# Interleaving the DRAM operands of an RWKV-7 mixer's batches, and loading them several tiles per transfer

## The chip, the cores and the metric

The kernel runs on one NeuronCore of a Trainium2 chip, with its five instruction streams: TensorE (PE, whose weight loads the profile lists apart as PEld), VectorE (DVE), ScalarE (ACT), GpSimd (POOL) and SyncE (SP), which in this kernel issues nearly all DMAs. Sixteen DMA engines move the data. The metric is the device time of one execution in microseconds (us); smaller is better. Everything below is float32 (or its rounded form fp32r for the large matmuls).

## What is computed

Two layers of a streaming encoder are run for two request groups (a prompt of 16 learned tokens and 1024 others, and a sample of 64 tokens), which the kernel puts side by side as T = 1104 token columns. Layer 0 mixes tokens with a gated DeltaNet, layer 1 with RWKV-7 time mixing; after each mixer stands a SwiGLU block. The change is in layer 1's mixer alone. Its reference, cut to what matters:

```python
def rwkv_mixer(h, shift_buf, S0, mu, w0, ..., w_r, w_k, w_v, w_o, ln_w, ln_b):
    ...
    r, k, v = xr @ w_r, xk @ w_k, xv @ w_v
    ...
    def step(S, inp):
        d_t, kk_t, b_t, v_t, k_t, r_t = inp
        sa = jnp.einsum('bhij,bhj->bhi', S, -kk_t)
        S = S * d_t[:, :, None, :] + sa[..., :, None] * b_t[:, :, None, :] + v_t[..., :, None] * k_t[:, :, None, :]
        return S, jnp.einsum('bhij,bhj->bhi', S, r_t)
    S, y = lax.scan(step, S0.astype(f32), seq)
    ...
    bonus = jnp.sum(r * k * r_k, axis=-1, keepdims=True) * v
    y = y + bonus.reshape(B, T, D)
    y = (y * gate).astype(h.dtype) @ w_o
```

There are 16 heads of 64 features. The kernel doesn't scan token by token; it works in chunks of 64 tokens, with a triangular inverse per chunk and head.

## The kernel before, in words

Features lie on the 128 partitions: a feature tile f (0 to 7) holds two heads, one in partitions 0 to 63 (q = 0) and one in 64 to 127 (q = 1). Tokens lie along the free dimension, in three groups g of six chunks, 384 columns each. A **batch** is one group g with four feature tiles (hf = 0 or 1), so there are six batches, numbered 0 to 5, each of two halves of three chunks.

Layer 1's mixer runs in two parts. In `rwkv_a` four dense projections are computed, with 24 steps (8 feature tiles by 3 groups) each. What follows a step of the projection for k is `post_k` (line 1347): it loads A and the summed decays (tiles `l0` and `sw`), computes the scaled operands, and stores four tiles of 128 x 384 to DRAM: `PQ` (line 1371), `KR[0]` (1373), `BK[0]` = bh (1376) and `BK[1]` = kh (1378). Its tiles have two buffers each. What follows a step of the projection for v is `post_v` (line 1401): it loads pq, kh and rt (1405 to 1407), stores `KR[1]` (1409), `V` (1415) and `BV` (1417). Beside the second of these the first batch is prepared already (lines 1423 to 1427).

In `rwkv_b` the batches follow each other. In the weave of batch i (line 1775) run: `chain(i)`, the recurrence over the six chunks (line 1631); `build` of both halves of batch i + 1 (line 1487); `inverse(i + 1)` (line 1537); `grams(i + 2)` (line 1469), which feeds the inverse after it; and `tail(i - 1)` (line 1688), which norms, adds the bonus, multiplies by the gate and by w_o and adds to x. Batch 0 is different: it has three halves of `build` (0,1), (1,0) and (1,1), `grams(1)` with `inverse(1)`, and the gates of `gates` (line 1093), whose results are stored to `GT` at line 1119.

- `build`, for each of its four feature tiles: six transfers of half the partitions each (four for `bk`, which puts b and k of three chunks side by side, in swapped order in the two halves, line 1503; two for `kb`, line 1505) and one for V (line 1506). Then small matmuls (lines 1512, 1514) whose results DVE masks (1517, 1518); then six matmuls by the identity that turn b and k to token-major (line 1524, copied by ACT at 1525); then six that turn V (line 1531, copied into W by ACT at 1534).
- `inverse`: two copies on ACT and two on DVE gather the 32 x 32 blocks into `rdp`, a tile of its own (line 1543); DVE transposes it into `b32a` (line 1546); 31 steps of substitution follow on DVE with a share on POOL (lines 599, 601); DVE transposes the result twice, into a tile of the slot `b32b` (line 1552) and one of the slot `b32a` (line 1555); then for two sets of blocks come matmuls at line 1567, an ACT copy (1571), matmuls at line 1578 that read the `b32b` tile, and an ACT copy (1581).
- `tail`: it loads `BV` and `GT` (lines 1697, 1699), and for each of the eight output tiles x (line 1726), adds, and stores x (line 1733), as long as g is 0 or 1.

**What sets the order.** `weave` takes steps of its generators in turn by their weights, which gives the program order. The framework that builds the program then moves instructions of an engine against each other where data allow, so the order that ran is the trace's: the `rdp` copies of one inverse, for example, ran ahead of the last matmuls of the inverse before it. Each engine, and SP's queue, then goes strictly in that order: an SP transfer that waits for its data holds up all that are queued behind it. A slot with one buffer (`bufs=1`) can be written for its next use only when the last reader of its former use has ended.

Of the kernel before, what the change touches and what calls it, by code (L numbers as in the profile page):

```python
# [52 lines left out]
def tile_trunk(ctx, tc, *aps, stages=("gdn", "ffn0", "rwkv", "ffn1"), dbg=None):  # L53
# [1039 lines left out]
    def gates(tp, xp, dr):  # L1093
# [18 lines left out]
        for f in range(8):  # L1112
            for g, (c0, n) in enumerate(LIVE):
# [5 lines left out]
                nc.sync.dma_start(dr["GT"][f, :, (g + 1) * 384 - n:(g + 1) * 384], o[:, :n])  # L1119
# [26 lines left out]
    def rwkv_a(hnp, col, prm, pc, plb, dr, esb, esx, esg, pend, esP):  # L1146
        C = math.exp(-0.5)
        with ExitStack() as es0, ExitStack() as es:
# [198 lines left out]
            def post_k(ps, n, g, f):  # L1347
# [28 lines left out]
                nc.sync.dma_start(dr["BK"][0, f, :, cs], bh)  # L1376
                nc.vector.tensor_tensor(kh, k2, pi, ALU.mult)
                nc.sync.dma_start(dr["BK"][1, f, :, cs], kh)
# [16 lines left out]
            with ExitStack() as es, ExitStack() as es1:  # L1395
# [5 lines left out]
                def post_v(ps, n, g, f):  # L1401
# [4 lines left out]
                    nc.sync.dma_start(kh, dr["BK"][1, f, :, cs])  # L1406
# [10 lines left out]
                    nc.sync.dma_start(dr["BV"][f, :, cs], pq)  # L1417
# [27 lines left out]
    class batches:  # L1445
        def __init__(self, dr, tm):
# [8 lines left out]
            self.dp = tm.tile([P, 32, 32], F32, tag="rdp", bufs=1, name="rdp")  # L1455
            nc.gpsimd.memset(self.dp[:, 24:32], 0.0)
# [12 lines left out]
        def grams(self, i):  # L1469
# [3 lines left out]
            for ff in range(4):  # L1473
# [3 lines left out]
                nc.sync.dma_start(b1, self.dr["BK"][0, f, :, cs])  # L1477
# [9 lines left out]
        def build(self, i, half):  # L1487
# [4 lines left out]
            W = B["W"][half] = tz.tile([P, 2, 3, 4, 64], F32, tag=f"W{z}", bufs=1, name=uid("W"))  # L1492
            for ff in range(4):
                f = 4 * hf + ff
                kb = tz.tile([P, 2, 2, 192], F32, tag=f"kb{z}", bufs=4, name=uid("kb"))
# [3 lines left out]
                bk = tp.tile([P, 3, 2, 64], F32, tag="bk", bufs=3, name=uid("bk"))  # L1499
                V = tp.tile([P, 192], F32, tag="V", bufs=2, name=uid("V"))  # L1500
                for q, r in enumerate(HR):
                    for a in range(2):
                        nc.sync.dma_start(bk[r, :, a ^ q], self.dr["BK"][a, f, r, cs].rearrange("p (c t) -> p c t", t=64))
                for q, r in enumerate(HR):
                    nc.sync.dma_start(kb[r, q], self.dr["KR"][:, f, r, cs].rearrange("a p c -> p a c"))
                nc.sync.dma_start(V, self.dr["V"][f, :, cs])
# [15 lines left out]
                for j in range(3):  # L1522
                    for a in range(2):
                        nc.tensor.matmul(v[HR[a], j], bk[:, j, a], ident, start=True, stop=True)
                nc.scalar.copy(bt, v)
                yield
                ps = psB()
                for j in range(3):
                    c = slice(64 * j, 64 * j + 64)
                    for q, r in enumerate(HR):  # L1530
                        nc.tensor.matmul(ps[HR[1 - q], c], V[:, c], ident[:, r], start=True, stop=True)
# [427 lines left out]
```

## Time and profile before

| What | Value |
|---|---|
| Median of 3 runs | 3365.65 us (3364.24, 3365.65, 3377.66) |
| Span of the profiled execution, first to last instruction | 3360.1 us; the profile has nothing of what lies around it |
| PE, PEld, DVE, ACT, POOL busy | 94%, 89%, 76%, 46%, 11% of the span |
| Granted TensorE clock, mean | 0.968 |
| DMA: packets, bytes, mean rate | 543,905, 452.36 MB, 135 GB/s |
| SP's DMA queue, share of 16 engines | 43.1% |

A busy PE isn't a PE at its peak, since the ends of matmuls are modelled. A matmul of float32 appears as two MATMUL rows. Lines in the profile are those of the listing above; where a helper issues an instruction (lines 109 and 110 split a tile into two fp32r parts, 130 to 132 are the three matmuls of a split product), the line is the helper's. By the lines of the trace, the steps of `post_k` lie between about 1792 and 1919 us, those of `post_v` between 1919 and 2079, and the batches' weaves between about 2077 and 2560.

### The profile page before, as it was taken

Reading aid. Unit: us, or ns where it says so; the run is one execution under the profiler, and the core shown is the slowest. Engines: PE = TensorE matmul, PEld = TensorE weight load, DVE = VectorE, ACT = ScalarE, POOL = GpSimd, SP = SyncE. Lnnn points to the kernel's source line nnn. Section 1 sums busy time; section 2 is a strip of 40 time slices with the busy share of each in tenths; the row PEclk is TensorE's granted clock in tenths of the full one; section 3 lists DMA queues with packets and bytes.
Section 4 is the critical chain, followed back from the end, with each engine's and each line's share of the span. In section 5 each row is a group of like instructions: output and inputs, shape, how many; then the busy total and the mean of one; then the engine's idle time right before and its main releaser. Section 6 shows DMA issues by size and latency. Waiting matters only on the chain. (4 is left out here: it accounts for less than half of the span.)

```text
span 3360.1 us, 67649 instructions
## 1 busy us (share of the span) xinstructions
PE 3175.1 (94%) x26274; PEld 2982.5 (89%) x26274; DVE 2553.9 (76%) x5127; ACT 1557.9 (46%) x3134; POOL 383.9 (11%) x719
## 2 busy tenths in 40 slices
PE   7999999899899999999999889889999999999998
PEld 7888888798899999999988777777778999999998
DVE  6968778566787667766887883899976787877775
ACT  5765757444543333212687743444455443333112
POOL 1202022001300000000001130433300310000000
PEclk9989989899999999999999999898999999999999
DMA  5433432694332223522255877455555333325231
GB/s 167 114 91 89 113 89 76 221 301 147 114 107 84 78 78 125 169 79 89 75 172 168 289 232 238 136 152 157 167 188 179 105 96 95 95 92 177 85 98 61
DMA packets 543905, 452.36 MB, mean 135 GB/s; under 512 B 78377, under 2 KB 494930, under 8 KB 543458
## 3 DMA queue, kind: packets, MB, share of 16 engines
q1 hardware_dynamic: 538682, 445.61, 43.1%
q8 instruction: 207, 3.39, 0.4%
q10 hardware_dynamic: 4904, 2.43, 0.3%
q14 instruction: 112, 0.92, 0.1%
HBM read 306.86 MB, written 141.07 MB: 133 GB/s over the span
## 5 line engine op out<-in xcount | busy, mean ns | idle before, releaser
L311 PE MATMUL psA<-tc,sh 128*128 128x276 f32 (+1 forms) x1712 | 499.1, 292 | 19.0 <-DVE hs L319 9.4
L313 PE MATMUL psA<-tc,sl 128*128 128x276 f32 (+1 forms) x1712 | 498.7, 291 | 4.0 <-DVE sl L110 3.9
L312 PE MATMUL psA<-tc,sh 128*128 128x276 f32 (+1 forms) x1712 | 498.3, 291 | 0.3 <-DVE tc L110 0.2
L407 DVE TENSOR_TENSOR xT<-xT,psA 128x384 f32<-128x384 f32 (+3 forms) x496 | 252.9, 521 | 137.0 <-PE psA L132 135.2
L311 PEld LDWEIGHTS psA<-tc,sh 128*128 128x128 f32 x1712 | 326.0, 190 | 21.2 <-DVE hs L319 10.0
L109 ACT CAST wh<-raw 128x1024 fp32r<-128x1024 f32 x159 | 166.2, 1048 | 365.8 <-PE psA L131 269.7
L313 PEld LDWEIGHTS psA<-tc,sl 128*128 128x128 f32 x1712 | 325.3, 190 | 4.9 <-DVE sl L110 4.7
L312 PEld LDWEIGHTS psA<-tc,sh 128*128 128x128 f32 x1712 | 325.5, 190 | 1.2 <-DVE tc L110 0.9
L131 PE MATMUL psA<-hl,wh 128*128 128x384 f32 (+3 forms) x1024 | 326.4, 319 | 0.0
L130 PE MATMUL psA<-hh,wh 128*128 128x384 f32 (+3 forms) x1024 | 325.7, 320 | 0.0
L132 PE MATMUL psA<-hh,wl 128*128 128x384 f32 (+3 forms) x1024 | 325.3, 318 | 0.0
L130 PE MATMUL psA<-hnh,wh 128*128 128x384 f32 (+1 forms) x768 | 270.2, 352 | 5.4 <-ACT hnh L109 4.1
L131 PE MATMUL psA<-hnl,wh 128*128 128x384 f32 (+1 forms) x768 | 269.3, 351 | 2.0 <-DVE hnl L110 2.0
L132 PE MATMUL psA<-hnh,wl 128*128 128x384 f32 (+1 forms) x768 | 267.2, 348 | 0.0
L109 ACT CAST sh<-raw 128x512 fp32r<-128x512 f32 x202 | 124.6, 620 | 253.8 <-PE psA L312 237.8
L130 PE MATMUL psA<-mxh,wh 128*128 128x384 f32 (+1 forms) x672 | 223.4, 343 | 9.9 <-ACT mxh L109 5.6
L110 DVE TENSOR_TENSOR wl<-raw,wh 128x1024 fp32r<-128x1024 f32 x159 | 195.5, 1231 | 47.1 <-ACT wh L109 46.8
L131 PE MATMUL psA<-mxl,wh 128*128 128x384 f32 (+1 forms) x672 | 228.4, 342 | 2.8 <-DVE mxl L110 2.5
L132 PE MATMUL psA<-mxh,wl 128*128 128x384 f32 (+1 forms) x672 | 225.9, 338 | 0.8 <-DVE wl L110 0.8
L130 PEld LDWEIGHTS psA<-hh,wh 128*128 128x128 f32 x1024 | 192.1, 188 | 0.6 <-ACT hh L109 0.4
L132 PEld LDWEIGHTS psA<-hh,wl 128*128 128x128 f32 x1024 | 192.5, 188 | 0.1
L131 PEld LDWEIGHTS psA<-hl,wh 128*128 128x128 f32 x1024 | 192.3, 188 | 0.3
(480 smaller groups left out, 8342.3 us busy)
## 6 DMA issues: line engine op xcount, KB each, us to landing
raw<-in_ffn_w_gate_dram SPq DMA_DIRECT2D x64, 512.0 KB
raw<-in_ffn_w_up_dram SPq DMA_DIRECT2D x64, 512.0 KB
raw<-in_ffn_w_down_dram SPq DMA_DIRECT2D x44, 512.0 KB
raw<-in_gdn_w_in_dram SPq DMA_DIRECT2D x32, 512.0 KB
raw<-in_gdn_w_out_dram SPq DMA_DIRECT2D x24, 512.0 KB
raw<-in_rwkv_w_o_dram SPq DMA_DIRECT2D x24, 512.0 KB
hr<-dhid SPq DMA_DIRECT2D x44, 276.0 KB
hr<-dhid SPq DMA_DIRECT2D x44, 272.0 KB
```

Of the source, the lines that this page charges most:

```text
L109: nc.scalar.copy(h, src)
L110: (eng or nc.vector).tensor_tensor(l, src, h.bitcast(F32), ALU.subtract)
L130: nc.tensor.matmul(ps, w[0][:, k, :], x[0][:, k, :n], start=a, stop=False)
L131: nc.tensor.matmul(ps, w[0][:, k, :], x[1][:, k, :n], start=False, stop=False)
L132: nc.tensor.matmul(ps, w[1][:, k, :], x[0][:, k, :n], start=False, stop=z)
L311: nc.tensor.matmul(ps, u[0][:, kk], h, start=first and kk == 0, stop=False)
L312: nc.tensor.matmul(ps, u[0][:, kk], l, start=False, stop=False)
L313: nc.tensor.matmul(ps, u[1][:, kk], h, start=False, stop=last and kk == 3)
L407: nc.vector.tensor_tensor(xT[:, m, a:a + n], xT[:, m, a:a + n], pd[:, :n], ALU.add)
```

## The change

1. **b and k interleaved in DRAM.** `BK` was [2, 8, 128, 1152] (b or k; tile; partition; token). It becomes [8, 128, 18, 2, 64]: for each chunk of 64 tokens b and k stand next to each other, in swapped order for the upper half of the partitions, as `build` wants them. A store of bh or kh in `post_k` becomes two stores of 64 partitions, each of six runs of 256 bytes a partition; the load of kh in `post_v` and that of b in `grams` become two such loads each.
2. **`build` loads several tiles at a time.** `bk` and V are loaded for two feature tiles per transfer (V has a second small transfer that repeats its first 64 columns at the end), `kb` for all four feature tiles of a half in four transfers of half the partitions.
3. **Transpose mode.** b and k are turned by three 128 x 128 transposes instead of six matmuls; V by three instead of six; ACT copies V's result in three pieces instead of two.
4. **`BV` and `GT` become one DRAM tile `BG`**, which `tail` loads with one transfer for two tiles.
5. **`tail` moves x two tiles at a time**, and a store is issued one step later.
6. **`rdp` loses its own tile.** It takes the slot `b32b`, and its last part is cleared by POOL in every inverse.

The diff, cut to its core:

```diff
@@ post_k
-                nc.sync.dma_start(dr["BK"][0, f, :, cs], bh)
+                for q, r in enumerate(HR):
+                    nc.sync.dma_start(dr["BK"][f, r, 6 * g:6 * g + 6, q], c3(bh)[r])
                 nc.vector.tensor_tensor(kh, k2, pi, ALU.mult)
-                nc.sync.dma_start(dr["BK"][1, f, :, cs], kh)
+                for q, r in enumerate(HR):
+                    nc.sync.dma_start(dr["BK"][f, r, 6 * g:6 * g + 6, 1 - q], c3(kh)[r])
@@ post_v
-                    nc.sync.dma_start(kh, dr["BK"][1, f, :, cs])
+                    for q, r in enumerate(HR):
+                        nc.sync.dma_start(c3(kh)[r], dr["BK"][f, r, 6 * g:6 * g + 6, 1 - q])
@@ batches
-            self.dp = tm.tile([P, 32, 32], F32, tag="rdp", bufs=1, name="rdp")
-            nc.gpsimd.memset(self.dp[:, 24:32], 0.0)
@@ grams
-                nc.sync.dma_start(b1, self.dr["BK"][0, f, :, cs])
+                for q, r in enumerate(HR):
+                    nc.sync.dma_start(b1[r].rearrange("p (c t) -> p c t", t=64), self.dr["BK"][f, r, 6 * g:6 * g + 6, q])
@@ build
+            kbs = tz.tile([P, 4, 2, 2, 192], F32, tag=f"kb{z}", bufs=1, name=uid("kb"))
+            for q, r in enumerate(HR):
+                for a in range(2):
+                    nc.sync.dma_start(kbs[r, :, q, a], self.dr["KR"][a, f0:f0 + 4, r, cs].rearrange("f p c -> p f c"))
             for ff in range(4):
+                if ff % 2 == 0:
+                    fs = slice(f0 + ff, f0 + ff + 2)
+                    bks = tp.tile([P, 2, 384], F32, tag="bk", bufs=2, name=uid("bk"))
+                    nc.sync.dma_start(bks, self.dr["BK"][fs, :, 6 * g + 3 * half:6 * g + 3 * half + 3]
+                                      .rearrange("f p c a t -> p f (c a t)"))
+                    Vs = tp.tile([P, 2, 256], F32, tag="V", bufs=2, name=uid("V"))
+                    v = self.dr["V"][fs, :, cs].rearrange("f p c -> p f c")
+                    nc.sync.dma_start(Vs[:, :, 0:192], v)
+                    nc.sync.dma_start(Vs[:, :, 192:256], v[:, :, 0:64])
...
                 for j in range(3):
-                    for a in range(2):
-                        nc.tensor.matmul(v[HR[a], j], bk[:, j, a], ident, start=True, stop=True)
+                    nc.tensor.transpose(v[:, j], bk[:, j].rearrange("p a t -> p (a t)"), ident)
...
                 for j in range(3):
-                    c = slice(64 * j, 64 * j + 64)
-                    for q, r in enumerate(HR):
-                        nc.tensor.matmul(ps[HR[1 - q], c], V[:, c], ident[:, r], start=True, stop=True)
-                for q in range(2):
-                    o = HR[1 - q]
-                    nc.scalar.copy(W[o, q, :, ff], ps[o, :192].rearrange("p (c t) -> p c t", t=64))
+                    nc.tensor.transpose(v[:, j], V[:, 64 * j:64 * j + 128], ident)
+                nc.scalar.copy(W[0:64, 1, :, ff], v[0:64, :, 64:128])
+                nc.scalar.copy(W[64:128, 0, 1:3, ff], v[64:128, 0:2, 0:64])
+                nc.scalar.copy(W[64:128, 0, 0, ff], v[64:128, 2, 0:64])
@@ inverse
+            dp = tp.tile([P, 32, 32], F32, tag="b32b", bufs=1, name=uid("rdp"))
+            nc.gpsimd.memset(dp[:, 24:32], 0.0)
@@ tail
-                    nc.sync.dma_start(bv[:, :n], dr["BV"][f, :, cs])
-                    nc.sync.dma_start(gt[:, :n], dr["GT"][f, :, cs])
+                    nc.sync.dma_start(bg[:, :, :n], dr["BG"][:, f, :, cs].rearrange("a p c -> p a c"))
...
+                    if g < 2:
+                        xt = tp.tile([P, 2, 384], F32, tag="xt", bufs=2, name=uid("xt"))[:, :, :n]
+                        nc.sync.dma_start(xt, dr["X"][:, xs, c0:c0 + n])
...
+                        if late:
+                            nc.sync.dma_start(*late)
+                            late = None
                         yield
+                    if g < 2:
+                        late = dr["X"][:, xs, c0:c0 + n], xt
```

More of the change, by code (lines that the diff above doesn't have):

```diff
@@ L1695, in tail @@
                     f = 4 * hf + ff
[L1696 to L1699 removed]
+                    bg = tp.tile([P, 2, 384], F32, tag="lbg", bufs=lb, name=uid("lbg"))
+                    nc.sync.dma_start(bg[:, :, :n], dr["BG"][:, f, :, cs].rearrange("a p c -> p a c"))
                     pc_ = psC()
@@ L1721, in tail @@
                     wv = [t.rearrange("p (k m) c -> p k m c", m=2) for t in u]
-                    for mm in range(2):
-                        m = 2 * mp + mm
-                        if g < 2:
-                            xt = tp.tile([P, 384], F32, tag="xt", bufs=4, name=uid("xt"))[:, :n]
-                            nc.sync.dma_start(xt, dr["X"][:, m, c0:c0 + n])
-                        else:
-                            xt = xT[:, m, c0:c0 + n]
+                    xs = slice(2 * mp, 2 * mp + 2)
+                    if g < 2:
+                        xt = tp.tile([P, 2, 384], F32, tag="xt", bufs=2, name=uid("xt"))[:, :, :n]
+                        nc.sync.dma_start(xt, dr["X"][:, xs, c0:c0 + n])
+                    else:
+                        xt = xT[:, xs, c0:c0 + n]
+                    for mm in range(2):
                         ps = psC()
                         mm3(ps[:, :n], (wv[0][:, :, mm], wv[1][:, :, mm]), yy, range(4), n)
-                        nc.vector.tensor_tensor(xt, xt, ps[:, :n], ALU.add)
-                        if g < 2:
-                            nc.sync.dma_start(dr["X"][:, m, c0:c0 + n], xt)
+                        nc.vector.tensor_tensor(xt[:, mm], xt[:, mm], ps[:, :n], ALU.add)
+                        if late:
+                            nc.sync.dma_start(*late)
+                            late = None
                         yield
+                    if g < 2:
+                        late = dr["X"][:, xs, c0:c0 + n], xt
+                if late:
+                    yield
+                    nc.sync.dma_start(*late)
             def first(tp, hp):
@@ L1906, in tile_trunk @@
     if "rwkv" in stages:
-        rs_ = {k: dp_.tile([8, P, 1152], F32, name="r" + k) for k in ("V", "GT", "BV", "R")}
-        for k in ("KR", "BK"):
+        rs_ = {k: dp_.tile([8, P, 1152], F32, name="r" + k) for k in ("V", "R")}
+        rs_["BK"] = dp_.tile([8, P, 18, 2, 64], F32, name="rBK")
+        for k in ("KR", "BG"):
             rs_[k] = dp_.tile([2, 8, P, 1152], F32, name="r" + k)
```

26 lines of the change are left out of this document (9 added, 17 removed).

## The prediction

> **What bounds the kernel now.** I read the page first, then the busy time by stage, then each stage's own limit.
>
> ```profile
> span 3360.1 us, 67649 instructions
> PE 3175.1 (94%) x26274; PEld 2982.5 (89%) x26274; DVE 2553.9 (76%) x5127; ACT 1557.9 (46%) x3134; POOL 383.9 (11%) x719
> ```
>
> PE at 94% is a mean over stages; what the change touches lies between 1792 and 2485 us. The stage table has, for each stretch, the busy us of PE, PEld, DVE, ACT and POOL, then the granted clock, the DMA engines' share and GB/s:
>
> ```profile
> 1792.00:1858.00 66.00, 64.11 (x344) 57.06 (x345) 64.33 (x121) 61.13 (x131) 12.78 (x17) 1.00 0.63 204
> 1858.00:1911.40 53.40, 51.43 (x278) 46.64 (x277) 48.55 (x90) 41.79 (x87) 6.39 (x13) 1.00 0.88 289
> 1925.00:2077.00 152.00, 135.96 (x1124) 117.49 (x1122) 101.70 (x203) 57.56 (x115) 30.34 (x63) 0.99 0.79 242
> 2077.00:2183.00 106.00, 90.98 (x1591) 74.54 (x1589) 76.21 (x181) 45.06 (x105) 36.89 (x81) 0.86 0.51 147
> 2183.00:2476.00 293.00, 265.92 (x4703) 219.80 (x4703) 272.62 (x638) 130.95 (x290) 97.21 (x201) 0.94 0.53 153
> ```
>
> The reader is to see five stages with different limits. In the first stretch of `post_k` PE and DVE are both at 97%. In its second (13 of its 24 steps) PE is at 96%, and the DMA engines at 88%. In `post_v` nothing is full (PE 89%, DMA 79%). In batch 0 (2077 to 2183) nothing is full either: PE is busy for 91 of 106 us, at a clock of 0.86. From 2183 on, batches 1 to 4, DVE is busy for 272.6 of 293 us in 638 instructions: what is left is 32 ns for each, so DVE hardly waits. Its waits there, longest first:
>
> ```profile
> DVE mb L1517 <- PE psB L1514: 2.8, 4, 1.1
> DVE b32a L1546 <- PE psB L1567: 1.9, 2, 0.9
> DVE xt L1731 <- PE psC L132: 1.7, 5, 0.6
> ```
>
> None of them names a DMA. The change takes nothing off DVE, so there its large saving on SP and its saving on PE mostly fall beside the path.
>
> **The change, part by part.** The prices of an issue on SP are these (ns: least, median, most):
>
> ```profile
> L1503 SPq DMA_DIRECT2D bk<-rBK x192: 573/606/1930, 1940.1 to 2462.8; - x192
> L1378 SPq DMA_DIRECT2D rBK<-kh x24: 320/407/580, 1807.2 to 1918.6; - x24
> L1406 SPq DMA_DIRECT2D kh<-rBK x24: 319/406/582, 1920.2 to 2062.7; - x24
> L1505 SPq DMA_DIRECT2D kb<-rKR x64: 573/607/1800, 2081.6 to 2449.7; - x64
> L1506 SPq DMA_DIRECT2D V<-rV x48: 319/537/1777, 1960.4 to 2468.7; - x48
> ```
>
> A transfer over half the partitions (bk, kb) takes 0.61 us, one over all of them 0.40 to 0.54.
>
> *`build` on SP.* A half of a batch issues 4 x (4 x 0.606 + 2 x 0.607 + 0.537) = 16.7 us. Afterwards it issues four of kb at 0.607, two of bk and four of V at 0.32 to 0.54 (I take 0.43): 5.0 us. That is 11.7 us less, 140 us over twelve halves. Where this counts is batch 0, which has three halves (35 us less of SP in 106). There SP goes from one issue to the next with gaps of 0.04 to 0.1 us:
>
> ```profile
> 2143.40 1.73 SPq L1503 DMA_DIRECT2D bk<-rBK  x2
> 2145.23 0.54 SPq L1119 DMA_DIRECT2D rGT<-go  x1
> 2145.82 0.58 SPq L1503 DMA_DIRECT2D bk<-rBK  x1
> 2146.44 1.26 SPq L1505 DMA_DIRECT2D xT<-rKR  x2
> ```
>
> *The transposes.* The rows are start and duration; what a burst costs PE is the distance to the next row's start:
>
> ```profile
> 136.10 0.49 PE L797 MATMUL psB<-ident,sil 128*128 128x128 f32 x3
> 136.34 0.40 PE L131 MATMUL psA<-hnl,wh 128*128 128x336 f32 x1
> ...
> 2488.22 0.88 PE L1524 MATMUL psB<-ident,bk 128*64 128x128 f32 x12
> 2488.93 0.52 PE L1531 MATMUL psB<-ident,V 128*64 128x64 f32 x12
> 2489.27 0.64 PE L1648 MATMUL psA<-W,kb 128*64 128x64 f32 x16
> ```
>
> Line 797 is three transposes of this size elsewhere in the kernel: 0.24 us. The two bursts they replace take 0.71 and 0.34. So a tile and half saves 1.05 - 2 x 0.24 = 0.57 us of PE: 27 us over 48, of which 6.8 in batch 0 (12 of them), 18 in batches 1 to 4, 2.3 in `post_v`.
>
> *Batch 0's sum.* Below: nothing, if its latencies set its length. Above: PE is left with 91.0 - 6.8 = 84.2 us; if it then ran without a gap, 22 us are gained. I take 10, the PE saving and 3 us of late operands: PE's waits there that name SP's loads or no releaser at all (an operand's landing, I take it) are these.
>
> ```profile
> PE psB L1531 <- issue: 2.7, 2, 1.7
> PE psB L1483 <- DMA k<-rKR: 1.0, 2, 0.7
> ```
>
> *Batches 1 to 4.* Only what DVE waits for PE can come back, 6.4 us in the rows above: from 0 to 6, I take 3.
>
> *`post_k` pays.* One step on SP, with the first store of the next:
>
> ```profile
> 1874.65 0.32 SPq L1371 DMA_DIRECT2D rPQ<-pq  x1
> ...
> 1876.04 0.40 SPq L1378 DMA_DIRECT2D rBK<-kh  x1
> ...
> 1876.99 0.44 SPq L1351 DMA_DIRECT2D sw<-rSW  x1
> 1878.47 0.32 SPq L1371 DMA_DIRECT2D rPQ<-pq  x1
> ```
>
> SP is taken for 2.8 us (1874.65 to 1877.43) in a step that lasts 53.4 / 13 = 4.1 in this stretch. Two issues of 0.40 become four of 0.61: 1.6 us more, 4.4 in all, over 4.1. Ahead of the two loads there are now 1.6 us more of stores. The DMA engines, too, get more to do:
>
> ```profile
> DMA packets 11209, 15.41 MB, mean 289 GB/s; under 512 B 1236, under 2 KB 11205, under 8 KB 11205
> q1 hardware_dynamic: 11205, 15.36, 87.5%
> ...
> DMA packets 539, 0.14 MB, mean 39 GB/s; under 512 B 535, under 2 KB 539, under 8 KB 539
> q1 hardware_dynamic: 539, 0.14, 17.1%
> out_dram<-so SPq DMA_DIRECT2D x1, 128.0 KB
> ```
>
> The first two rows are the 53.4 us of these 13 steps: 0.875 x 16 x 53.35 us / 11,205 = 66.7 ns a packet, nearly all of 1.5 KB. The last three are 3.5 us around a lone store of 256-byte rows: 0.171 x 16 x 3.5 us / 539 = 17.8 ns a packet. A step's 256 packets of 1536 bytes (17.1 us of engine time) become 1536 of 256 bytes (27.3): 0.64 us more over 16 engines, which brings 87.5% of 4.1 us to 4.2 us, 103%. So both SP and the DMA engines pass the step's length by 0.1 to 0.3 us: 4 us over the 13 steps. The other 11 steps are longer (the ten in the first stretch take 6.6 us) and have room. Bounds: nothing, if the loads are ordered ahead of the stores and the tiles' second buffers absorb it; 24 x 1.6 = 39 us, if all comes in series. I take 7: the 4, and some of the later loads.
>
> The Trainium skill, "DMA: Bandwidth & Descriptors", section Specifications, says that transfers below 512 bytes aren't at line rate because the DMA engine then reads, modifies and writes. The row of the lone store shows 17.8 ns for 256 bytes against 66.7 for six times as much: less efficient by 1.6, with no second pass to be seen.
>
> *`post_v`.* kh costs SP two issues of 0.61 for one of 0.41, 0.8 us in each of 24 steps, b1 likewise in eight of its 24 uses, and `build` (0,0) gives back 11.7 there. DVE's product waits for pq and rt, which stand beside kh in the queue. From 8 us gained (PE's 2.3 and half of the 11.7) to 19 lost; I take 2 lost, as SP has idle time here and PE 11%.
>
> *The slot of `rdp`.* At the handover from batch 3 to 4:
>
> ```profile
> 2391.33 1.67 ACT L1543 COPY rdp<-at 32x768 f32<-32x768 f32 x2
> 2395.64 1.11 DVE L1543 COPY rdp<-at 32x768 f32<-32x768 f32 x2
> 2402.56 0.95 PE L1567 MATMUL psB<-b32tn,at 32*32 32x32 f32 x48
> 2403.55 2.09 DVE L1546 STREAM_TRANSPOSE b32a<-rdp 128x1024 f32<-128x1024 f32 x1 [0.94 <-PE psB L1567]
> 2406.56 0.95 PE L1578 MATMUL psB<-b32tt,v 32*32 32x32 f32 x48
> ```
>
> The copies ran 8 us and more ahead, and the transpose waited only for line 1567 (the other slot). Now the copies must wait for the end of line 1578 at 2407.5, the last reader of `b32b`; with ACT's two, 1.67 us side by side with DVE's 1.11, the transpose comes at 2409.2: 5.7 us later. Queued behind DVE's copies are all of DVE's masks and the tail's additions, unless ordered ahead. There are four such handovers, 23 us if DVE stood still. DVE has other work, by its rows at least half of the stretch, so I take 8. If the filling work is ready, nothing is lost.
>
> *The rest at nothing.* ACT's third copy (48 more, ACT under 50% busy), POOL's clearing (POOL busy 97 of 293), `tail`'s fewer transfers and later stores (SP only, under a DVE that is full). If that cover were gone, the copies would cost 48 times some 0.2 us, 10 us.
>
> Sum: -10 - 3 + 7 + 2 + 8 = +4 us. The profiled span of 3360.1 lies 5.6 below the median of the runs, 3365.65, with nothing shown of what lies around it; I add the sum to the median: **3370 us**.
>
> **The rivals.** A measurement of this kernel can tell about 0.5%, 17 us, from no change.
>
> *Two: SP's queue is what holds the batches.* For it: SP's back-to-back issues, and that batch 0 is the longest though no engine is full. Then batch 0 gains the 22, batches 1 to 4 the 6, the handovers and `post_v` come free, and 7 are paid: -21, 3345. Against it: few waits name a DMA.
>
> *Three, slower: `post_k` becomes bound by its stores.* It decides where SP's 4.4 us pass the step's 4.1. If the loads stand behind the four half stores in every step, the whole 1.6 us come in series: 39 in place of 7, 3402. Against it: double buffers, and ten steps with room.
>
> *Four: a 256-byte store costs twice*, 35.6 ns, because its bytes move twice. Then 13 steps hold 13 x (54.7 - 17.1) / 16 = 30.6 us more of DMA time on 46.7, 77 us for 53.4: +24 in place of 7, 3387. The lone store speaks against it. It is what the rule of the Trainium skill above (same page and section) would give.
>
> *Five: the handovers cost their full 23*, +15 over mine: 3385. For it: DVE's order is fixed, so a copy that waits stops DVE.
>
> **How the numbers follow.** Forecast 0.45, two 0.27, three 0.13, four 0.03, five 0.12. The forecast's own range is where its terms stay within the bounds of no change, 3350 to 3382. Two lies faster by over 0.5% (3349). Three and four lie above 3382; five straddles it, 0.07 above. Faster 0.27, same 0.50, slower 0.23. The range reaches down past two's 3345, and up through five to half of three: 3338 to 3392.
>
> **What would show it.** Right: batch 0 about 96 us instead of 106; a step of `post_k` at 4.3 to 4.9 us instead of 4.1, DMA share there over 0.93, SP back to back; the transposes 0.25 us a burst of three; line 1546 waiting for ACT's or DVE's copies after line 1578. Wrong: `post_k`'s stretch at its old length (then SP and DMA had room), batches 1 to 4 shorter by over 10 us (then DVE wasn't the bound), or 256-byte stores well over 18 ns.

## The result, and the profile after

The changed kernel takes 3471.52 us (median of 4 runs, 3470.92 to 3476.48), the kernel before on the same chip 3366.11 (4 runs, 3364.24 to 3377.66). The ratio is 1.0293, with a 95% interval of 1.0273 to 1.0313: about 105 us slower, where 4 us were forecast and the range ended at 3392.

The page of the kernel after, its first lines:

```profile
span 3469.6 us, 65672 instructions
...
PE 3204.5 (92%) x25410; PEld 2994.8 (86%) x25410; DVE 2553.2 (74%) x5127; ACT 1563.2 (45%) x3182; POOL 384.7 (11%) x724
```

PE's busy time grew by 29 us (3175.1 to 3204.5), that of its weight loads by 12 and no other engine's by more than 6, while the span grew by 109.5: most of it is waiting. Two rows mark where: the stores of PQ, one in each step of `post_k`, and the copies at the head of each chain (line 1638 before, 1646 after). Each row has the count, the durations (ns: least, median, most), and the first and last start. First the kernel before:

```profile
L1371 SPq DMA_DIRECT2D rPQ<-pq x24: 319/320/524, 1791.7 to 1914.0; - x24
L1638 DVE COPY W<-Sk x8: 275/288/293, 2080.4 to 2400.0; 64x256 f32<-64x256 f32 x8
L1638 DVE COPY xT<-Sk x4: 274/286/293, 2078.7 to 2245.1; 64x256 f32<-64x256 f32 x4
```

Then the kernel after:

```profile
L1371 SPq DMA_DIRECT2D rPQ<-pq x24: 319/326/573, 1785.6 to 1980.0; - x24
L1646 DVE COPY W<-Sk x8: 285/288/292, 2188.4 to 2500.0; 64x256 f32<-64x256 f32 x8
L1646 DVE COPY xT<-Sk x4: 285/291/481, 2186.4 to 2348.6; 64x256 f32<-64x256 f32 x4
```

They cut the span into stages, and the same rows of every later kernel cut its span in the same way: `post_k` from the first to the last PQ store; `post_v` from there to the first copy of chain 0 (2078.7 before); the chains from there to the last copy (2400.0); and the rest. Changes of the length: up to the first PQ store -6.1 us, `post_k` +72.1 (122.3 to 194.4), `post_v` +41.7 (164.7 to 206.4), the chains -7.7 (321.3 to 313.6), the rest +9.5 (960.1 to 969.6). Two stages lost 113.8 us, and both are those in which the interleaved tile is written or read by halves (the Gram products of the later batches, within the chains, read it so too). Each stage length is that of one profiled execution, and such an execution lay up to 13 us from its kernel's median (3450.79 for 3463.8 in one case below), so a difference of under some 10 us in a stage may be chance.

The busy time in `post_k`'s second stretch and in `post_v`, kernel after (columns as in the prediction):

```profile
1850.00:1980.00 130.00, 87.54 (x374) 77.56 (x373) 83.34 (x149) 74.08 (x143) 5.71 (x17) 0.78 0.60 166
1980.00:2186.40 206.40, 148.08 (x1020) 125.07 (x1021) 96.09 (x184) 47.25 (x97) 30.76 (x69) 0.80 0.65 190
```

In `post_k`'s second stretch, where PE stood at 96% and the DMA engines at 88%, PE now has 67%, the DMA engines 60%, and the granted clock fell to 0.78. Neither of them is full there, nor is DVE (64%). What SP does in it:

```profile
1908.93 0.32 SPq L1371 DMA_DIRECT2D rPQ<-pq  x1
1909.35 0.38 SPq L1373 DMA_DIRECT2D rKR<-pe  x1
1909.82 1.25 SPq L1377 DMA_DIRECT2D rBK<-bh  x2
1911.17 1.26 SPq L1380 DMA_DIRECT2D rBK<-kh  x2
1913.03 0.33 SPq L1371 DMA_DIRECT2D rPQ<-pq  x1
...
1913.92 1.25 SPq L1377 DMA_DIRECT2D rBK<-bh  x2
1915.27 1.26 SPq L1380 DMA_DIRECT2D rBK<-kh  x2
1916.58 1.11 SPq L1341 DMA_DIRECT2D l<-rA  x1
1917.73 0.43 SPq L1351 DMA_DIRECT2D sw<-rSW  x1
1918.20 0.43 SPq L1341 DMA_DIRECT2D l<-rA  x1
1918.68 0.43 SPq L1351 DMA_DIRECT2D sw<-rSW  x1
1923.11 0.32 SPq L1371 DMA_DIRECT2D rPQ<-pq  x1
```

The reader is to see two things. A half store costs 0.63 us, as priced. But the order is another: the stores of two steps, then the loads of two steps, then 4.0 us in which SP waits (1919.11 to 1923.11) for ACT's pq of the next pair. In the kernel before each step's stores are followed by one pair of loads. The same pairing stands in the order in which the built program has ACT's instructions (number = step, counted from 1; sq three times a step, at lines 1353, 1356 and 1357):

```
before  sq11 k9 sq11 sq11 pe9 pi9 pq9 sq12 k10 sq12 sq12 pe10 pi10 pq10 sq13 k11 sq13 sq13 pe11 pi11 pq11
after   sq12 sq12 sq12 sq13 sq13 sq13 k9 pe9 pi9 pq9 k10 pe10 pi10 pq10 sq14 sq14 sq14 sq15 sq15 sq15 k11
```

Before, a step's three sq instructions are mixed with the other instructions of an earlier step; after, ACT does two steps' sq and then two steps' rest. DVE's order is paired likewise.

What this costs shows on PE, the fullest engine of the second stretch before. From the first to the last PQ store PE is idle for 47.5 of 194.4 us, before for 5.2 of 122.3. Its longest waits from 1850 to 1985 us, kernel after:

```profile
PE psA L130 <- DVE k L1361: 22.9, 7, 7.3
PE psA L130 <- ACT wh L109: 13.4, 1, 13.4
```

Line 1361 is the last reader of the projection's result. It needs ACT's k (line 1360), which in the new order stands behind the sq of two steps, and PE waits for it before it goes on with the projection; in the kernel before no wait of PE in this stage names it. The second row is a weight of v's projection that was loaded late. The other 29.8 us of the 72.1 are busy time of PE, 146.9 us in 668 rows after and 117.1 in 624 before: a row takes 220 ns on average instead of 188, at a granted clock of 0.83 instead of 1.00 in the stage. How much of the loss the clock makes by itself, no run here separates.

### The profile page after: what moved, and what is told of

Same layout as the page of the kernel before. It is cut to its first block, busy times and chain, and to the rows that moved or that the text cites. A ratio compares the mean times of both kernels' runs of the same rounds, so it can differ in the third digit from the quotient of the medians.

```text
span 3469.6 us, 65672 instructions
## 1 busy us (share of the span) xinstructions
PE 3204.5 (92%) x25410; PEld 2994.8 (86%) x25410; DVE 2553.2 (74%) x5127; ACT 1563.2 (45%) x3182; POOL 384.7 (11%) x724
## 4 chain that ended last, share of the span: by engine, by line
PE 72%; DVE 14%; ACT 5%; DMA 4%; issue 3%; POOL 1%; SPq 1%; DVEq 0%; ACTq 0%; POOLq 0%
PE psA L131 9%; PE psA L130 9%; PE psA L132 9%; PE psA L311 8%; PE psA L313 8%; PE psA L312 8%; DVE b32t L601 2%; PE psC L130 2%; DVE b32u L599 2%; PE psC L132 2%; PE psC L131 2%; POOL cs L285 1%; DVE acc L767 1%; PE psC L783 1%; DVE wl L110 1%
## 5 line engine op out<-in xcount | busy, mean ns | idle before, releaser
L130 PE MATMUL psA<-mxh,wh 128*128 128x384 f32 (+1 forms) x672 | 236.1, 360 | 48.3 <-DVE k L1361 25.5
L131 PE MATMUL psA<-mxl,wh 128*128 128x384 f32 (+1 forms) x672 | 239.3, 358 | 0.9 <-DVE mxl L110 0.7
```

The source lines that it names most:

```text
L130: nc.tensor.matmul(ps, w[0][:, k, :], x[0][:, k, :n], start=a, stop=False)
L131: nc.tensor.matmul(ps, w[0][:, k, :], x[1][:, k, :n], start=False, stop=False)
```

## The experiments

Two theories stood against each other from here on. *Price*: the half stores and short rows cost this time themselves, in SP's queue, the DMA engines or the landing. *Order*: they cost little, but the framework that orders the instructions puts them otherwise because of them. All stage lengths are read from the two rows named above; ratios are to the kernel before on the same chip.

**Undo the layout.** The changed kernel with b and k in two tensors again, whole stores, and everything else of the change but `build`'s loads of b and k, which need the layout: eight transfers of half the partitions fill a tile in place of one:

```diff
-                for q, r in enumerate(HR):
-                    nc.sync.dma_start(dr["BK"][f, r, 6 * g:6 * g + 6, q], c3(bh)[r])
+                nc.sync.dma_start(dr["BK"][0, f, :, cs], bh)
...
-                    nc.sync.dma_start(bks, self.dr["BK"][fs, :, 6 * g + 3 * half:6 * g + 3 * half + 3]
-                                      .rearrange("f p c a t -> p f (c a t)"))
+                    for q, r in enumerate(HR):
+                        for a in range(2):
+                            for i in range(2):
+                                nc.sync.dma_start(bkv[r, i, :, a ^ q], self.dr["BK"][a, f0 + ff + i, r, cs].rearrange("p (c t) -> p c t", t=64))
```

> The changed kernel with part 1 of the change undone: BK keeps its old layout, bh and kh are stored, and kh and b loaded, whole; build's two-tile bk tile is filled by eight half-partition transfers; all the rest of the change stays. Every theory has the loss in part 1. It should bring the post_k stretch from 198 us back to about 127 and the post_v stretch from about 200 back to about 150, so 3355 to 3370 us. If the other parts cost anything by themselves (the shared slot of rdp, the 8 us per handover that the prediction charged), it stays above 3375; if they gain, as batches 1 to 4 of the changed kernel did (8 us shorter), it lands at 3350 to 3362.

Measured: 3368.61 us, ratio 0.9976 (0.9962 to 0.999). `post_k` 124.5, `post_v` 170.2, the chains 322.4, the rest 965.2. The layout, with the transfers that depend on it, carries the whole loss; the rest of the change gains 0.2%, less than can be told from no change in one comparison, though the interval excludes 1. The chains' 7.7 us go with the layout too.

**Load a step ahead, with a third buffer** for `l0` and `sw`, in the changed kernel:

```diff
-                A = load("l0", "A", f, g)
-                sw = tmp("sw", [P, 390])
-                nc.sync.dma_start(sw, dr["SW"][f, :, 6 * g:6 * g + 6].rearrange("p a b -> p (a b)"))
+                A, sw = ahead.pop(0)
+                fetch()
```

> The changed kernel, all of its transfers kept, but the loads of A and the decays for post_k are put one step further ahead in the program, with a third buffer each, so that each step's stores are followed by one pair of loads and not two steps' stores by two pairs. Theory of order: the loss in post_k comes from loads that stand behind two steps' stores in SP's queue; the stretch falls from 198 us to 125 to 150, the time to 3400 to 3425. Theory of price: the half-partition stores of 256-byte runs are slow by themselves; the stretch stays above 175 us and the time above 3445.

Measured: 3452.15 us, ratio 1.0231 (1.0209 to 1.0253): some 20 of the 105 us came back. `post_k` takes 164.2, between what the two theories had foretold, while the time lies above the 3445 of *price*. Most of what is left of the stage's loss is one stall. The waits of PE in that stage:

```profile
PE psA L130 <- ACT wh L109: 30.6, 1, 30.6
```

A weight for the projection came late, as its load stood far behind in SP's queue. One order was mended and another one spoilt. `post_v`, with no edit of its own, got 8 us longer (214.3).

**The halves alone, and the short rows alone**, each put into the kernel before. The first stores bh and kh in two halves with the old layout and long rows:

```diff
-                nc.sync.dma_start(dr["BK"][0, f, :, cs], bh)
+                for r in HR:
+                    nc.sync.dma_start(dr["BK"][0, f, r, cs], bh[r])
```

> The kernel before with one edit: each store of bh and kh is made as two stores of 64 partitions, in the old layout with its long rows of 1536 bytes. Theory of order: the queue's order is regrouped by the two additional issues alone, and post_k's stretch goes from 127 us to 165 to 200, the time to 3400 to 3440. Theory of price by small rows: no 256-byte row is in it, so the stretch stays under 140 us and the time under 3380. Theory of SP's issue time alone: 24 steps by at most 0.8 us, under 3390.

The second keeps one store for 128 partitions, in rows of 256 bytes side by side (all loads of b and k follow the new layout):

```diff
-                nc.sync.dma_start(dr["BK"][0, f, :, cs], bh)
+                nc.sync.dma_start(dr["BK"][f, :, 6 * g:6 * g + 6, 0], c3(bh))
```

> The kernel before with one edit: b and k interleaved in DRAM (not swapped), so bh and kh are stored, and kh and b loaded, in 256-byte rows, each by one transfer over all 128 partitions; build's transfers keep their number. Theory of order: the queue is regrouped here too, so post_k takes 165 to 200 us and the time is 3400 to 3440. Theory of SP's issue time: no issue is added, so the time stays under 3380. Theory of price by small rows: the time rises by most of the 105 us.

Measured, one run each: 3426.1 and 3423.96 us. `post_k` takes 176.1 and 166.3, that is 54 and 44 us more than before, `post_v` 164.8 and 170.8. Either edit by itself costs most of what the two do together, and the second adds no issue at all to SP. In the time of the second stretch of before, 1858 to 1911.4, the DMA engines are busy for 0.56 and 0.61, not 0.88. And the two built programs, which share no edit, have the same order of `post_k`'s instructions on ACT, and all but the same on DVE, largely in pairs. That made the theory of the order the first.

**SP's order held.** The changed kernel, with order edges (each puts one instruction behind another in the built program) that keep SP in the sequence of before:

```diff
+                    with tc.issue_after(prev[0]) if prev[0] else ExitStack():
+                        A = load("l0", "A", f, g)
+                        sw = tmp("sw", [P, 390])
+                        prev[1] = nc.sync.dma_start(sw, dr["SW"][f, :, 6 * g:6 * g + 6].rearrange("p a b -> p (a b)")).ins
...
-                nc.sync.dma_start(dr["PQ"][f, :, cs], pq)
+                with tc.issue_after(prev[1]), tc.issue_after(prev[2]) if prev[2] else ExitStack():
+                    nc.sync.dma_start(dr["PQ"][f, :, cs], pq)
```

> The changed kernel with every transfer of post_k kept (four half stores of 256-byte rows in a step), but SP's queue held by order edges to the order of the kernel before: stores of one step, then the two loads of the step after next, then stores of the next step; the last weights are loaded as early as in the kernel before. Theory order (the loss in post_k is the planned order, which puts the loads of two steps behind the stores of both): post_k from first to last PQ store takes 125 to 140 us instead of 195 (123 before), SP back to back at about 4.4 to 5 us a step, and the kernel about 60 us less than after's 3471: 3405 to 3420. Rival theory price (half stores of 256-byte rows are dear in themselves, in SP, DMA engines or landing): post_k stays at 165 us or more, the kernel at 3440 or more. Both: post_v is not touched, and stays near 206 us up to the first copy of chain 0.

(`prev[0]` is the last store of the step before, `prev[1]` the load of sw, `prev[2]` that of a weight.)

Measured: 3467.84 us, ratio 1.0276 (1.0247 to 1.0304); `post_k` 186.0. By the numbers on record that is the answer of *price* (165 or more, 3440 or more), and the theory of order in this form, the order of SP's stores and loads, fell. One part of it is a stall: a weight came late in spite of the edges, since they hold what follows a weight's load and not the load itself. PE's row after it:

```profile
1867.69 0.65 PE L132 MATMUL psA<-mxh,wh 128*128 128x336 f32 x1 [24.35 <-ACT wh L109]
```

But the 13 steps after that stall also take 6.7 to 8.0 us each, with SP idle in them. SP of this kernel, the end of one step and the next two stores of PQ:

```profile
1906.84 1.26 SPq L1394 DMA_DIRECT2D rBK<-kh  x2
...
1908.81 0.43 SPq L1358 DMA_DIRECT2D sw<-rSW  x1
1912.17 0.32 SPq L1385 DMA_DIRECT2D rPQ<-pq  x1
```

and ACT in the same time:

```profile
1907.72 0.58 ACT L1366 ACTIVATE sq<-psA,prm 128x384 f32<-128x384 f32 x1 [2.20 <-PE psA L134]
1909.31 0.58 ACT L1369 ACTIVATE sq<-psC,eps_t 128x384 f32<-128x384 f32 x1 [1.00 <-PE psC L1368]
1909.79 0.70 ACT L1373 ACTIVATE k<-l,ka,prm 128x384 f32<-128x384 f32 x1
...
1911.63 0.51 ACT L1381 ACTIVATE pq<-sw 128x384 f32<-128x384 f32 x1
```

SP waits 2.9 us for pq (1909.24 to 1912.17). pq of this step comes after k (line 1373) in ACT's order, and k stands behind lines 1366 and 1369 of a later step, for which ACT waited 2.20 and 1.00 us. In the order of before, k stands ahead of the second of these. So ACT's order was still another than before, and held SP up.

**The same with `post_v`**, whose four loads of a step were also held ahead of the stores of the step before:

> As the kernel with the old order in post_k, and post_v's four loads of a step are traced one step ahead and held together behind the last store of the step before last. Theory order, which says that post_v too loses by its queue's order (the second half of kh stands behind stores that wait for DVE): post_v up to chain 0 falls from 206 to 165 to 180 us and the kernel to 3365 to 3385. Rival theory price: post_v stays at 195 to 210, the kernel no better than the one with post_k alone in the old order. A third way: the forced order is itself a bad one, with BG's store at its end (pq's load then waits for that store's landing), and post_v gets longer.

Measured: 3463.8 us, ratio 1.0254 (1.0222 to 1.0286); `post_k` 185.9, `post_v` 199.6, where the changed kernel has 206.4 and the run above 210.5. Little came back in this form either, and `post_v` is where *price* had it (195 to 210).

**One order on four engines, with the old transfers and with the new.** `post_k` was rewritten as a pipeline by hand: the sum of squares of a step stands in the middle of the next step's matmuls, the rest of the step after it, and each instruction of SP, ACT and DVE, with PE's sum of squares, is tied to the one before it on its engine; the weights are loaded early. This was done to the kernel before (the control) and to the changed one, so that the two differ in `post_k` by its transfers.

```diff
+            def chain(fn, *a, **kw):
+                e = fn.__self__
+                with tc.issue_after(last[e]) if e in last else ExitStack():
+                    last[e] = fn(*a, **kw).ins
...
+                                mm3(ps[:, :n], u, m[g], range(4), n, last=False)
+                                hook.pop()()
+                                with tc.issue_after(mml[0]):
+                                    mm3(ps[:, :n], u, m[g], range(4, KT), n, first=False)
```

> The kernel before, with post_k written as a pipeline by hand and the order of its instructions on SP, ACT, DVE and PE held by order edges (first half of a step's matmuls, then the last step's sum of squares, and so on); transfers as before. It is the control of the next kernel: post_k at 110 to 140 us (123 in the kernel before), and the whole within 20 us of 3372. If a hand-made order is bad in itself, post_k shows it here.

> The changed kernel with the same hand-held order of post_k's instructions on SP, ACT, DVE and PE, and its four half stores of 256-byte rows in every step. Theory plan (the loss in post_k is not the stores' price but the order in which the compiler then puts the instructions of ACT and DVE, in pairs of steps, which the earlier run left free while it held only SP's): post_k is 5 to 25 us longer than the control's, SP at 4.4 to 4.9 us a step the most that the stores can ask; with post_v at its 237 us from the last PQ store to batch 1 the kernel at about 3410 to 3425. Rival theory price (the stores themselves cost it: issue, queues or landing): post_k again 60 us or more longer than the control's, the kernel at 3455 or more.

Measured: the control 3376.47 us, ratio 1.0005 (0.9992 to 1.0018), `post_k` 112.3; the changed transfers 3445.2 us, ratio 1.0201 (1.0174 to 1.0227), `post_k` 140.2. Against the changed kernel's 194.4 the held order gave back 54 us, against 10 in the control. What is left between the two, 27.9 us, is the price of the transfers under one order (18.0 by the time of the last PQ store, 1938.8 against 1920.8). The two later pairs below, with the same order in `post_k`, show 30.8 (142.2 and 111.4) and 30.7 (142.1 and 111.4). So the other 41 to 44 of the 72 belong to the order, if the transfers cost the same under both. On record the order theory had 5 to 25 us and 3410 to 3425, the price theory 60 us or more and 3455 or more: both were missed, the stage nearer the first, the time between the two. SP in the kernel with the new transfers:

```profile
1886.08 0.38 SPq L1361 DMA_DIRECT2D rPQ<-pq  x1
...
1887.02 1.28 SPq L1361 DMA_DIRECT2D rBK<-bh  x2
1888.39 1.28 SPq L1361 DMA_DIRECT2D rBK<-kh  x2
1889.73 0.60 SPq L1361 DMA_DIRECT2D l<-rA  x1
1890.38 0.44 SPq L1361 DMA_DIRECT2D sw<-rSW  x1
1890.91 0.38 SPq L1361 DMA_DIRECT2D rPQ<-pq  x1
```

Here, and not in the kernel as it was changed, is what the prediction said: SP goes from one issue to the next, 4.83 us a step, 4.4 for the issues and 0.4 for eight gaps. (All held instructions have the line of the helper, 1361; one goes by the tiles.) Behind this queue the loads land late. The waits for them from 1850 us on to the last PQ store, control first:

```profile
DVE sw L1361 <- DMA sw<-rSW: 3.7, 5, 1.1
ACT k L1361 <- DMA l<-rA: 3.6, 6, 1.3
```

and with the new transfers:

```profile
ACT k L1361 <- DMA l<-rA: 17.2, 12, 2.0
DVE sw L1361 <- DMA sw<-rSW: 14.0, 12, 1.7
```

24 us more of such waits, in a stage that is 28 longer; the two engines may wait at the same time, so this is no account.

**The same order in the changed kernel without the layout**, to see whether the hand-made order is worth having:

> The changed kernel without the new layout of b and k (whole stores, long rows, as in the kernel that undid the layout and measured 0.998 of before), with the same hand-held order in post_k. If that order is at least as good as the compiler's: post_k as in the control, the kernel at 3355 to 3372. If it is worse than the compiler's, it shows in post_k and in the control alike.

Measured: 3376.17 us, ratio 1.0005 (0.999 to 1.0021); `post_k` 111.4. The time is above the 3372 that was foretold for an order as good as the framework's. The 10 to 13 us that the hand-made order takes off `post_k` don't appear in the whole, here or in the control: the first PQ store comes 16 to 17 us later (1807.5 and 1808.5 for 1791.7), since a step's stores here follow the next step's first half.

**`post_v`: the half loads alone.** The kernel before with kh and b loaded in two halves of long rows:

```diff
-                    nc.sync.dma_start(kh, dr["BK"][1, f, :, cs])
+                    for r in HR:
+                        nc.sync.dma_start(kh[r], dr["BK"][1, f, r, cs])
```

> The kernel before, with only the loads of kh in post_v and of b in the Gram products in two halves of 64 partitions (old layout, long rows, stores untouched). If the split loads alone give the 41 us that post_v lost: from the last PQ store to chain 0 about 195 to 206 us instead of 165, the kernel at 3400 to 3410. If they don't (the 41 come from the layout or from build's place in the queue): 165 to 175, and the kernel within 10 us of the one before. The prediction's own term was 2 us, from 8 gained to 19 lost with all of post_v's edits. post_k unchanged at 123.

Measured, one run: 3401.66 us; `post_v` 182.5, 17.8 more than before, and the chains 331.6. The stage lies between the two answers (the time is that of the first, but 10 us of it stand in the chains): the halves alone, with whatever order they bring, are worth less than half of the 41.7. They may be worth less still: with none of these loads changed, `post_v` takes 174.0 in the kernel of `rdp`'s slot below.

**`post_v` with its SP order held**, with the old transfers and the new, on top of the one order in `post_k`: KR, pq of the next step, V, BV, then kh and rt of the step after next, and the weights early.

> The control of the one order in post_k, with post_v's SP instructions held as well: stores and loads of a step in the kernel before's sequence (KR, pq of the next step, V, BV, then kh and rt of the step after next), and its weights loaded early; transfers as before. From post_k's last PQ store to the first chain 155 to 175 us (165 in the kernel before and in the control); the whole 3365 to 3385.

> The changed kernel with the one order in post_k and post_v's SP instructions held in the same sequence as in the control of this run, kh as two half loads of 256-byte rows. Theory plan (post_v too lost its 41 us to an order in which a step's loads stand just before they are needed): from post_k's last PQ store to the first chain at most 20 us more than in the control of this run, 165 to 190, and the kernel at 3395 to 3420. Rival theory price (two half loads for one, and short rows, are dear whatever the order): 200 us or more, as in the changed kernel with post_k alone held (213.6), and the kernel at 3430 or more.

Measured: 3378.59 us, ratio 1.0008 (0.999 to 1.0026), and 3442.3 us, ratio 1.0185 (1.0154 to 1.0215); `post_v` 165.0 and 202.6, a difference of 37.6. By the words on record that is the answer of *price* (200 or more, 3430 or more). But the loads of the Gram products stood elsewhere in the two queues. So those were held as well, with the loads of `build` and of the gates:

> The control again, now with every SP instruction of post_v's stretch in one written order: also the loads of the Gram products, of build and of the gates, all four of b and k in a block behind step 6; transfers as before. That block stops SP while it waits for PE to free a slot, in this kernel as in the next: from the last PQ store to the first chain 165 to 185 us.

> The changed kernel with SP's order of post_v's stretch written out as in this run's control. Theory plan: what is left of post_v's loss is where the compiler put the loads of the Gram products, build and gates; then this kernel is at most 20 us longer than its control from the last PQ store to the first chain, whatever the control takes. Theory price (half loads and short rows): again 35 us or more above the control, and no less than the 202.6 of the run before.

Measured, one run each: 3375.71 and 3433.94 us; `post_v` 181.8 and 214.3, a difference of 32.5. By the words on record that is neither theory's: more than 20, less than 35. The trace shows what is in it. The first weights of v's projection stand behind `post_k` in the program and were not held. Their loads, with the new transfers, and the row of PE that waited for them:

```profile
L122 SPq DMA_DIRECT2D raw<-in_rwkv_w_v_dram x3: 373/617/634, 1949.7 to 1961.0; - x3
```

```profile
1959.67 0.65 PE L135 MATMUL psA<-mxh,wh 128*128 128x336 f32 x1 [27.09 <-ACT wh L109]
```

and the same two in the control:

```profile
L122 SPq DMA_DIRECT2D raw<-in_rwkv_w_v_dram x5: 383/432/454, 1903.0 to 1922.7; - x5
```

```profile
1910.51 0.65 PE L135 MATMUL psA<-mxh,wh 128*128 128x336 f32 x1 [4.09 <-ACT mxh L109]
```

The control has the first weight loaded 11.3 us before its last PQ store (1914.3), the other 3.6 us after its own (1946.1); PE stands for 27.09 us instead of 4.09. From PE's first matmul of that projection to chain 0 it is 185.6 us (1910.5 to 2096.1) in the control and 200.7 (1959.7 to 2160.4) with the new transfers: 15.1 more. In the pair of runs before, whose rows show the same stall (26.66 and 4.09), it is 168.8 and 189.1: 20.3 more. So 15 to 20 us are left as the price of the transfers in `post_v`, about as much as the half loads alone showed (17.8), if the stall is counted to the order, as the place of the weights in SP's queue suggests; no run with those weights held shows it. Even this is not free of order. The block of the Gram products' loads with the new transfers, and then in the control:

```profile
1996.65 0.61 SPq L1462 DMA_DIRECT2D k<-rKR  x1
2001.52 1.25 SPq L1462 DMA_DIRECT2D b<-rBK  x2
```

```profile
1955.25 0.38 SPq L1460 DMA_DIRECT2D k<-rKR  x1
1956.30 0.32 SPq L1460 DMA_DIRECT2D b<-rBK  x1
```

The third load of b waits for the first product to free its slot: 4.3 us in the one, 0.7 in the other, and all of `post_v`'s transfers wait behind it. In the built program the first Gram product stands 31 of the projection's matmuls behind PE's last sum over kh in the one, 7 in the other. PE's order there was not held, and holding every engine in `post_v`, beside the inverse and `build`, wasn't tried.

**The slot of `rdp` alone**, in the kernel before:

```diff
-            self.dp = tm.tile([P, 32, 32], F32, tag="rdp", bufs=1, name="rdp")
+            dp = tp.tile([P, 32, 32], F32, tag="b32b", bufs=1, name=uid("rdp"))
+            nc.gpsimd.memset(dp[:, 24:32], 0.0)
```

> The kernel before, with only rdp taken from the slots of b32b (line 1546's copies must wait for the readers of the slot) and POOL's clearing of it each batch. The prediction priced the four handovers at 8 us, bounds 0 and 23: 3374, all of it between chain 0 and the end. Rival: other work fills them, 0, and the kernel within 4 us of the one before.

Measured: 3368.36 us, ratio 0.9978 (0.9961 to 0.9995); the chains 321.3, as before. The handovers cost nothing that shows. `post_v` takes 174.0 in its profiled execution, 9.3 more than before, which wasn't looked into.

The fastest of all is the first, the change without its layout, at 0.9976.

## Why the prediction was wrong, point by point

- **`post_k`: +7 forecast, +72.1 measured. This is the step that failed.** It said: "Bounds: nothing, if the loads are ordered ahead of the stores and the tiles' second buffers absorb it; 24 x 1.6 = 39 us, if all comes in series." Both ends hold the order of the instructions fixed and price the new issues in it. The order didn't stay: SP, ACT and DVE now do the steps in pairs, and no engine or queue is full while they do: PE, idle for 5.2 us of the stage before, is idle for 47.5, mostly behind DVE's k and one late weight. Under one order on four engines the price is 27.9 to 30.8 us, inside the bounds, though nearer rival three's 39 than the 7 that were taken; the 41 to 44 beyond lay outside any bound given. SP's 4.4 us a step (4.83 with its gaps) and a half store's 0.61 (0.63) were right.
- **`post_v`: +2 forecast (-8 to 19), +41.7 measured.** The same step, missed in the same way: the loads were priced one by one, in an order taken for given. The price by the held pairs is 15 to 20 us, at the upper bound, and the half loads alone cost up to 17.8. The rest is put down to order, which is argued and not shown: in the held pairs 23 us of it are the wait for the projection's late weights; in the changed kernel that wait is 13.4 us and stands in `post_k`'s stage. What PE waits for in `post_v` itself is DVE's product with kh, before and after:

```profile
PE psC L1412 <- DVE kh L1410: 10.9, 10, 2.1
PE psC L1415 <- DVE kh L1413: 36.0, 14, 6.3
```

The reason that the prediction gave, DVE's product waiting for loads that stand beside kh in the queue, was right in kind: after, DVE waits 35.5 us for the load of rt, before 7.6 (and 13.2 for pq).
- **Batch 0: -10 forecast, -1.3 measured** (2078.7 to 2161.1 before, 2186.4 to 2267.5 after, by the first copies of the chains; the forecast's stretch went on to 2183). SP was relieved, and nothing came of it: rival two, that SP's queue holds the batches, falls as well. The saving on the transposes is there. PE's groups of lines 1524 and 1531, kernel before:

```profile
L1524 PE MATMUL psB<-ident,bk 128*64 128x128 f32 x576 | 47.1, 285 | 6.2 <-DVE kb L1518 3.8 <-DVE xT L1518 2.5
L1531 PE MATMUL psB<-ident,V 128*64 128x64 f32 x576 | 29.7, 237 | 4.3 <-issue 4.3
```

and their successors after:

```profile
L1537 PE MATMUL psB<-ident,V 128*128 128x128 f32 x114 | 22.3, 298 | 9.0 <-issue 3.6 <-ACT bt L1532 2.6 <-ACT xT L1532 2.2
L1531 PE MATMUL psB<-ident,bk 128*128 128x128 f32 x114 | 20.8, 293 | 0.6 <-DVE xT L1526 0.4 <-DVE kb L1526 0.3
```

76.8 us busy became 43.1, or 54.4 if the 30 records of 144 that are missing in each group are counted like the others: 22 to 34 us less, 27 forecast. It didn't shorten PE's work in batch 0: between the two first copies PE is busy for 69.3 of 82.4 us before and 70.3 of 81.1 after, and why wasn't looked into.
- **Batches 1 to 4: -3 forecast (0 to -6), -6.4 measured** (238.9 to 232.5 from the second chain's first copy to the last copy). The whole chains, batch 0 among them, take 307.1 to 318.0 us in the seven kernels with the change's layout (mean 312.0), and 313.9 to 333.7 in the nine with the old one (mean 325.0; the kernel of the short rows is left out). So the gain is there on average, is more likely above the bound of 6 than below it, and comes with the layout and the loads that need it, not with the transposes: the two kernels in which only these were undone have 322.4 and 333.7.
- **The handovers of `rdp`: +8 forecast (0 to 23), nothing measured.** In the kernel after, line 1554 (1546 before) waits this long for the copies:

```profile
  ACT rdp L1551: 0.7, 2
```

That DVE had other work, as the prediction's own term assumed, fits this; rival five, the full 23, falls.
- **The rest: 0 forecast, +9.5 measured** between the two profiled executions. The other kernels with the change's layout have 964.7 to 971.3 there, those with the old one 962.3 to 965.4: about 5 us, not looked into.
- **Rival four: a 256-byte store costs twice.** The transfers of 70 us of `post_k` in the kernel with SP's order held:

```profile
DMA packets 21675, 11.76 MB, mean 168 GB/s; under 512 B 16632, under 2 KB 21671, under 8 KB 21671
...
q1 hardware_dynamic: 21671, 11.71, 60.2%
```

0.602 x 16 x 70 us are 674 us; the 5039 longer packets at the 66.7 ns of before take 336, and 16,632 short ones the other 338: 20 ns each, not 35.6. To hold this rival for unlikely was right. The rule of the Trainium skill ("DMA: Bandwidth & Descriptors", Specifications), that transfers below 512 bytes are read, modified and written, would double it; no run here shows it in the packets' time.

Of the signs named beforehand, "SP back to back" and a DMA share over 0.93 failed in the changed kernel (0.60), as did a step of 4.3 to 4.9 us (a pair of steps took 14.2 in the rows above), and that was what told the cause apart: a stage got longer while what should have bound it stood idle.

Why the framework chose pairs is argued, not shown: it orders by its own estimates, and two quite different edits that it may both take for dear gave the same order.

## What to carry to other kernels

Where a framework orders the instructions, the price of an edit is the price of its operations plus that of the order that comes with them, and the second can be the larger: 41 to 44 of 72 us here. Read the built program's order of each engine before and after, ahead of any sum, and if the steps are grouped otherwise, bound the stage by a trace that has such a grouping, not by the old one. To tell the two apart on the chip, hold one order on all engines that take part, with the old and with the new operations; holding one queue alone moved 8 us of 72, and each load that was not held found another late place.

## What the runs showed that was not expected

A lone change of row length, with no issue added, cost a stage 44 us while its DMA engines were less busy than before (0.61 for 0.88 in the same stretch). And in the stages in which PE waits more, the granted clock is lower: 1.00 and 0.99 in most of `post_k` and `post_v` before, 0.78 and 0.80 after, though PE had less to do in each us. In the changed kernel's `post_k` the matmuls of 128x336 that follow a wait of 3.07 us start 0.28 us apart from 1908.47 to 1911.27, and 0.15 to 0.16 us apart after 1911.46. By this succession a wait costs PE more than its own length; that the wait is the cause is not shown, as no run tests it.
